# Loading five of 128 row tiles in pieces of 8, 112 and 8 rows in a DMA-bound rotation kernel

## Chip, cores and metric

One core of one Trainium2 chip. The metric is the device time of the whole kernel in microseconds. Of each kernel we quote the median of its runs and their range.

## The reference

```python
x = np.random.randn(8192, 8192).astype(np.float32)   # seeded
def reference(x, k):          # k = 1
    return np.rot90(x, k)
```

A matrix of 268 MB is read and 268 MB are written, turned by a quarter. There is no arithmetic.

## The kernel before

The input is cut into macro tiles of 1024 rows by 4096 columns (the last one into two of 512 rows). A macro tile is eight row tiles of 128 rows, 16 KB of each row. SP issues a load per row tile (128 in all); DVE reverses the columns of each 128-wide block on the way into chunk buffers; PE transposes blocks into PSUM; ACT copies PSUM to an output tile and issues the store.

```python
a_pool = ctx.enter_context(tc.tile_pool(name="a_pool", bufs=2))
r_pool = ctx.enter_context(tc.tile_pool(name="r_pool", bufs=63))
o_pool = ctx.enter_context(tc.tile_pool(name="o_pool", bufs=3))
# [cut]
def load(r0, rt, c0):
    nonlocal loads
    chunks = {}
    for t in range(rt):
        # [cut: a = a tile of 128 x 4096 from a_pool or, at the start, o_pool]
        loads += 1
        nc.sync.dma_start(
            out=a[:], in_=x[r0 + t * P : r0 + (t + 1) * P, c0 : c0 + W]
        )
        for j in range(W // CH):                 # CH = 512: 8 chunks
            ar = r_pool.tile([P, CH // P, P], dt, tag="ar")
            nc.vector.tensor_copy(out=ar[:], in_=...)   # columns reversed
            chunks[t, j] = ar
        yield chunks
```

There are 63 chunk buffers where a macro tile has 64 chunks, so the loads of the next macro tile follow closely on PE's transposes of this one.

## Time and profile before

| | before |
|---|---|
| time, median of 3 (range) | 1267.88 us (1267.56 to 1267.9) |
| span of the profiled run | 1265.8 us |
| bytes in and out | 268.44 + 268.44 MB |
| loads / stores | 128 / 129 |

The prediction below shows the lines of the page that carry the argument: the DMA row is full and the queues' shares add up to all 16 DMA engines. From the page, what the DMA engines moved in 40 equal slices of 31.6 us, and the two main groups of DMA issues with their KB and median us from issue to landing:

```profile
GB/s 398 426 429 429 428 429 429 428 431 427 429 429 429 428 430 429 429 428 429 429 429 428 429 421 430 427 430 429 423 429 428 418 429 428 428 429 425 428 422 334
...
out_dram<-ot ACTq DMA_DIRECT2D x127, 2048.0 KB, 25.6
a<-in_x_dram SPq DMA_DIRECT2D x128, 2048.0 KB, 16.7
```

428 to 430 GB/s is what this mix of loads and stores reaches when nothing is in its way. The table of stretches where the 25th tile will be loaded (the columns: stretch, its length, busy us and count of PE, PE weight loads, DVE, ACT and POOL, granted clock, DMA share, GB/s):

```profile
188.00:192.00 4.00, 0.00 (x0) 0.00 (x0) 0.00 (x0) 0.00 (x0) 0.00 (x0) 0.52 1.02 434
192.00:196.00 4.00, 1.12 (x4) 0.72 (x4) 1.87 (x6) 0.66 (x1) 0.00 (x0) 0.50 0.99 422
196.00:203.00 7.00, 5.74 (x32) 5.74 (x33) 0.91 (x3) 4.84 (x3) 0.00 (x0) 0.58 1.01 433
203.00:207.00 4.00, 3.78 (x34) 3.42 (x32) 2.78 (x8) 1.87 (x1) 0.00 (x0) 1.00 0.98 418
207.00:211.00 4.00, 1.69 (x16) 1.58 (x15) 0.00 (x0) 3.50 (x2) 0.00 (x0) 1.00 1.04 438
```

And the waits for PE (us in total, times, longest), with the stretch of 20 us where one of the macro tiles changes:

```profile
ACT ot L164 <- PE pt L143: 247.7, 43, 17.3
...
750.00:770.00 20.00, 12.63 (x90) 11.87 (x88) 5.55 (x16) 8.92 (x6) 0.00 (x0) 0.84 1.01 419
```

### The profile page before, as it was taken

To read this page: it belongs to the slowest core of one execution; us is meant where nothing else is said; L and a number is where in the kernel's file an instruction comes from. 1 tells how busy PE (TensorE), PEld (TensorE's weight loads), DVE (VectorE), ACT (ScalarE), POOL (GpSimd) and SP (SyncE) were. 2 spreads that over 40 slices of the span, in tenths; PEclk is the share of its full clock that TensorE was granted. 3 is DMA by queue.
4 is the path that set the end of the run, shared out by engine and by line. 5 is a ranking of instruction groups with operands and counts; after the bars stand their busy time and mean duration, and the time that the engine had idled before them with its cause. 6 is when DMAs were issued, how large, how long until landed. Compare 5 with 4: busy or idle time off the path is not lost.

```text
span 1265.8 us, 10385 instructions
## 1 busy us (share of the span) xinstructions
PE 685.3 (54%) x4096; PEld 639.3 (51%) x4096; DVE 355.3 (28%) x1024; ACT 467.8 (37%) x257; POOL 0.7 (0%) x6
## 2 busy tenths in 40 slices
PE   1555545555555554564555546566464655546573
PEld 1544444554445454554545545565454655545572
DVE  4423322232222322232222322233222332223210
ACT  0433334333343333433424334243442434324363
POOL 0000000000000000000000000000000000000000
PEclk9977877768777777777777776776767776767777
DMA  9999999999999999999999999999999999999998
GB/s 398 426 429 429 428 429 429 428 431 427 429 429 429 428 430 429 429 428 429 429 429 428 429 421 430 427 430 429 423 429 428 418 429 428 428 429 425 428 422 334
DMA packets 37057, 537.55 MB, mean 425 GB/s; under 512 B 4112, under 2 KB 4112, under 8 KB 4112
## 3 DMA queue, kind: packets, MB, share of 16 engines
q10 hardware_dynamic: 18576, 268.44, 50.0%
q1 hardware_dynamic: 18432, 268.44, 49.8%
q8 instruction: 32, 0.52, 0.2%
q14 instruction: 17, 0.14, 0.0%
HBM read 268.44 MB, written 268.44 MB: 424 GB/s over the span
## 4 chain that ended last, share of the span: by engine, by line
DMA 77%; ACT 8%; DVE 8%; PE 5%; issue 1%; ACTq 0%; DVEq 0%; SPq 0%
DMA a<-in_x_dram 48%; DMA out_dram<-ot 30%; ACT ot L164 8%; DVE ar L106 8%; PE pt L143 5%; ACTq L172 0%; DVEq L106 0%; ACTq L164 0%; SPq L101 0%
## 5 line engine op out<-in xcount | busy, mean ns | idle before, releaser
L143 PE MATMUL pt<-ident,ar 128*128 128x128 f32 x4096 | 685.3, 344 | 560.7 <-ACT ot L164 396.1
L143 PEld LDWEIGHTS pt<-ident,ar 128*128 128x128 f32 x4096 | 639.3, 183 | 606.5 <-ACT ot L164 433.2
L164 ACT COPY ot<-pt 128x2048 f32<-128x2048 f32 x256 | 466.5, 1869 | 755.5 <-DMA out_dram<-ot 506.3
L106 DVE COPY ar<-a 128x512 f32<-128x512 f32 x1024 | 355.3, 422 | 865.4 <-DMA a<-in_x_dram 827.9
L164 ACT ACT_TABLE_LOAD x1 | 1.3, 1283 | 25.6 <-DVE ar L106 25.6
masks.py:199 POOL TENSOR_SCALAR_AFFINE_SELECT ident<-ident 128x128 f32<-128x128 f32 x1 | 0.3, 292 | 0.1
masks.py:197 POOL MEMSET ident<- 128x128 f32 x1 | 0.2, 204 | 0.3 <-POOLq L212 0.3
L212 POOL MEMSET const-bfloat16-1.0<- 128x1 bf16 x1 | 0.1, 102 | 0.0
L212 POOL MEMSET const-uint8-127<- 128x1 uint8 x1 | 0.1, 102 | 0.0
L212 POOL MEMSET const-float32-0.0<- 128x1 f32 x1 | 0.1, 99 | 0.2 <-issue 0.2
L212 POOL MEMSET const-float32-1.0<- 128x1 f32 x1 | 0.1, 99 | 0.0
## 6 DMA issues: line engine op xcount, KB each, us to landing
a<-in_x_dram SPq DMA_DIRECT2D x128, 2048.0 KB, 16.7
out_dram<-ot ACTq DMA_DIRECT2D x127, 2048.0 KB, 25.6
out_dram<-ot ACTq DMA_DIRECT2D x2, 1024.0 KB, 14.9
```

What stands on the lines that cost most here:

```text
L106: nc.vector.tensor_copy(out=ar[:], in_=a[:, j * CH : (j + 1) * CH].rearrange("r (b m) -> r b m", m=P)[:, :, ::-1],)
L143: nc.tensor.transpose(ps[w // PW][:, PW - 1 - w % PW, t * P : (t + 1) * P], chunks[t, g * P // CH][:, g % (CH // P), :], ident,)
L164: nc.scalar.copy(o[:, G - PW - h : G - h, :], ps[h // PW])
L212: nc = _bacc.Bacc("TRN2", target_bir_lowering=False, num_devices=1)
```

## The change

With 8 + 112 + 8 rows, DMA engines 0 to 7 get nine rows of the tile and 8 to 15 get seven, in place of eight each; the prediction shows why. The intent, as far as it can be read, is to even out the DMA engines, which do not end together.

```diff
+EVERY = 25
+UNEVEN = [(0, 8), (8, P - 8), (P - 8, P)]
@@ in load()
             loads += 1
-            nc.sync.dma_start(
-                out=a[:], in_=x[r0 + t * P : r0 + (t + 1) * P, c0 : c0 + W]
-            )
+            for p0, p1 in UNEVEN if loads % EVERY == 0 else [(0, P)]:
+                r = r0 + t * P
+                nc.sync.dma_start(
+                    out=a[p0:p1, :], in_=x[r + p0 : r + p1, c0 : c0 + W]
+                )
```

## The prediction

> **What bounds the kernel now.** I read the page first: engine shares, slices, queues, chain.
>
> ```profile
> PE 685.3 (54%) x4096; PEld 639.3 (51%) x4096; DVE 355.3 (28%) x1024; ACT 467.8 (37%) x257; POOL 0.7 (0%) x6
> DMA  9999999999999999999999999999999999999998
> q10 hardware_dynamic: 18576, 268.44, 50.0%
> q1 hardware_dynamic: 18432, 268.44, 49.8%
> q8 instruction: 32, 0.52, 0.2%
> q14 instruction: 17, 0.14, 0.0%
> DMA 77%; ACT 8%; DVE 8%; PE 5%; issue 1%; ACTq 0%; DVEq 0%; SPq 0%
> ```
>
> No compute engine is over 54% busy. The DMA row is at 9 in 39 slices of 40, and the shares of the four queues add up to 100% of 16 engines' span: loads (q1) 49.8, stores (q10) 50.0, instruction fetches (q8, q14) 0.2. The chain of waits is 77% DMA. So the time is set by the 16 DMA engines, and work elsewhere is free as long as it feeds them.
>
> Next the table of stretches, to see where DMA is not full (columns: stretch, length, busy time and count of five engines, clock, DMA share, GB/s).
>
> ```profile
> 8.00:40.00 32.00, 7.77 (x28) 5.00 (x28) 18.45 (x54) 1.28 (x1) 0.00 (x0) 1.00 1.01 432
> 200.00:240.00 40.00, 22.54 (x158) 21.32 (x157) 11.10 (x32) 17.86 (x10) 0.00 (x0) 0.84 1.01 428
> 1180.00:1220.00 40.00, 23.64 (x130) 22.73 (x131) 11.75 (x36) 16.41 (x9) 0.00 (x0) 0.70 1.01 429
> 1220.00:1257.00 37.00, 22.37 (x192) 20.51 (x190) 0.72 (x3) 23.69 (x13) 0.00 (x0) 0.90 1.00 415
> 1257.00:1266.00 9.00, 0.00 (x0) 0.00 (x0) 0.00 (x0) 0.00 (x0) 0.00 (x0) 0.50 0.29 121
> ```
>
> Full from 8 to 1257 us, then 0.29 in the last 9: some engines are done while others work. That ragged end is all that balancing can win. I took it from the trace's own records. Each DMA posts 16 landings, one per engine. For the last store these come, after the first of them, at 0.0 (four), 0.1, 0.2, 1.0, 1.0, 1.7, 1.9, 1.9, 2.0, 2.1, 3.4, 5.6 and 6.5 us. The mean is 1.7 us, so perfect balance would save 6.5 - 1.7 = 4.8 us, 0.4%. No outcome near 2% faster is possible.
>
> Who is late? Packet records name no engine, but an engine's next packet starts 3 or 4 ns before its last ends, and each gets eight data packets and one semaphore write per DMA, so the records can be followed as 16 streams. My reconstruction gives: eight streams with the q8 fetches (32 of 16 KB, four each; this group ends with 0.2 to 3.4 us of lag); three of the other eight with all q14 fetches (7, 6 and 4 of 8 KB); five with none. The two that end last (6.5 and 5.6 us) are those with 7 and 6 q14 fetches. A q14 fetch takes 0.31 us and the packet after it about 1.2 instead of 0.61: 0.9 us. A q8 fetch takes 1.0 and the next packet 1.0: 1.4 us. The leaders sometimes run dry (near 675, 750, 907 and 986 us, about 0.1 us each time), because loads are released by the slowest engine's landing; the two laggards never wait. They are the bound.
>
> **What the Trainium skill says.** "DMA: Bandwidth & Descriptors", section "Why a DMA increments its semaphore by 16 and not by 1": the engine count is the largest number up to 16 that divides the slowest dimension, and on the hardware queues the lowest-numbered engines are taken. So 8 rows go to engines 0 to 7, one row each, and 112 rows to all 16, seven each. The trace of before agrees for 128 (16 landings per DMA, eight 16 KB packets each); 8 and 112 are not shown yet.
> "Runtime: NRT & Kernel Launch", section "Instruction fetch mechanics": instructions arrive in 16 KiB blocks by DMA queues of their own. The trace agrees: q8's 32 packets of 16 KB. It does not say which engines carry them.
> "SBUF — State Buffer", section "Door 1: The DMA port swizzle": partitions 0 to 3 share one port, 4 to 7 another, 120 to 123 and 124 to 127 two more, and four partitions alone got 27.6 GB/s. Before has no such case: each engine writes its own eight partitions of a 128-row tile (same DMA page, section "The descriptor swizzle"), and load packets show no slowing (0.611 us at the median and at the 90th percentile).
>
> **The change part by part.** Removed: five loads of 128 rows (the 25th, 50th, 75th, 100th and 125th; before, issued at 187, 433, 679, 925 and 1172 us). Added: 15 loads in their place. No PE, DVE or ACT instruction changes; the comparison of the two instruction orders shows only SP with more rows, 140 for 130. Costs:
> - Bytes. Engines 0 to 7 get 1 + 7 + 1 = 9 rows of such a tile, 8 to 15 get 7, instead of 8 each. One row is one packet of 0.611 us. Five tiles: +3.06 us on each of 0 to 7, -3.06 us on each of 8 to 15. Semaphore writes are 9 ns: ten more on 0 to 7, under 0.1 us.
> - Issue.
>
> ```profile
> L101 SPq DMA_DIRECT2D a<-in_x_dram x128: 327/328/534, 0.7 to 1201.1; - x128
> DMA to landing us min/median/max: 7.4/16.7/25.0
> ```
>
> Two more issues of 0.33 us put the last piece 0.66 us later. A load takes 16.7 us from issue to landing at a pace of one per 9.8 us, so its predecessor is still 6.9 us from landing at that moment. Hidden: 0.
> - Semaphores. The pieces use more of the eight DMA semaphores, so pieces two and three wait for earlier stores: for the first split tile those which before landed at 168.4 and 178.1 us, against an issue at 187.2. Checked for all DMAs of the program in the same way, no added wait ends after the old issue time. 0.
> - Writing 8 rows. Eight engines write to two ports. If the four on a port came together, 4 x 0.61 = 2.4 us would pass instead of 0.61, 1.8 us lost on each. But engines 0 to 7 are spread over a packet or more and alternate between loads and stores, so I estimate 0 to 1 us. The two laggards come 5 us after the others and can meet only each other: 0 to 0.6 us per piece, ten pieces, 0 to 6 us.
> - The 112 rows no longer lie engine by engine on its own port; a few packets may collide. Estimate 0 to 2 us over all five.
>
> So everything hangs on which half the two laggards are in. The change seems meant to relieve 8 to 15 of q8's fetches, which is the group of eight, 1.4 x 4 = 5.6 us against a relative shift of 2 x 3.06 = 6.1. In the very first load, the only moment when all engines start idle, the streams without q8 start early: places 1, 3, 4, 5, 7, 8, 9 and 11 of 16; the two laggards are third and fourth. If the order of start follows the engine number roughly, q8 is on 8 to 15 and the laggards, with their q14 fetches, are in 0 to 7. Then the change evens out the two halves on average and lengthens the two engines that end last: 1267.9 + 3.1 + (0 to 6) = 1271 to 1277.
>
> **The rivals.**
> (a) Laggards in 0 to 7, as just told. For: the order of first packets, and the author's choice of half. Against: that order is noisy (two q8 streams start second and sixth). +3.1 us without port contention, about +7 with it. I give it 0.6, half of that with contention.
> (b) q8 on 0 to 7, laggards in 8 to 15. The worst q8 engine has 3.4 + 3.06 = 6.5 us of lag, the laggards 6.5 - 3.06 = 3.4: the end stays at 6.5. 1268. Chance 0.15.
> (c) The halves are mixed, the laggards in 8 to 15 with the worst q8 engines. Best case: eight light engines in the lower half have at most 1.0 + 3.06 = 4.1 us, so the gain is 2.4; less when one with 2.1 us is among them (1.3). 1265.5 to 1266.6. For it: a kernel this tuned is seldom changed for nothing. Chance 0.25.
> (d) Full port contention on every piece, 1.8 us ten times: 1268 + 18 + 3 - 6 (the lead of the non-critical engines) = 1283. Against: the spread of the streams. It is the tail of (a).
>
> **Range and chances.** 0.3 x 1271 + 0.3 x 1275 + 0.15 x 1268 + 0.25 x 1266 = 1270.5. The low end, 1265.0, is just under the best of (c); the high end, 1278, takes in (a) with most of the contention. The repeats of before lie within 0.4 us, so noise adds nothing. Two per cent is 25 us: faster by that exceeds the 4.8 us there are; slower needs more than (d) in full. 0.01, 0.96, 0.03.
>
> **What would show it right or wrong.** The load queue should have 18432 packets plus the added semaphore writes; 268.44 MB as before; the first piece should post 8 landings, the second 16. If (a): the last store's landings keep two late streams, now some 9 us after the first unless leaders wait, and the DMA share of the last 9 us stays low. If (c): the spread of the last store shrinks to about 4 us. Contention: load packets of over 0.7 us in the five places, 8-row pieces slower than one packet time. If lanes matter after all: a DMA wait of SP over 12 us (the longest is 11.5 now), or DMA slices under 9 at 187 us and so on. I would be wrong altogether if the time fell below 1263, since that is more than the ragged end has to give, or rose past 1283.

## The result and the profile after

| | before | after |
|---|---|---|
| time, median of 6 (range) | 1267.82 us (1267.12 to 1267.9) | 1282.1 us (1279.8 to 1283.59) |
| ratio, 95% interval | 1 | 1.0111 (1.0098 to 1.0124) |
| span of the profiled run | 1265.8 us | 1280.1 us |

A ratio here and below is formed from the runs of the same rounds, so it is not quite the ratio of the medians quoted. The change costs 14.3 us, 1.1%. That is within 2%, but outside the predicted range of 1265 to 1278. The runs also scatter over 3.8 us, where those of before scatter over 0.8. All outputs are right.

The same lines of the page, after:

```profile
PE 688.8 (54%) x4096; PEld 640.3 (50%) x4096; DVE 355.2 (28%) x1024; ACT 468.1 (37%) x257; POOL 0.7 (0%) x6
GB/s 401 426 429 429 429 428 398 429 430 428 429 428 429 405 420 429 413 430 428 428 428 399 428 373 428 429 429 428 430 414 429 412 431 427 427 428 418 409 424 341
...
q1 hardware_dynamic: 18512, 268.44, 50.0%
q10 hardware_dynamic: 18576, 268.44, 49.7%
...
DMA 81%; DVE 12%; ACT 3%; PE 2%; issue 1%; ACTq 0%; DVEq 0%; SPq 0%
...
a<-in_x_dram SPq DMA_DIRECT2D x123, 2048.0 KB, 16.6
a<-in_x_dram SPq DMA_DIRECT2D x5, 1792.0 KB, 18.7
```

The kernel is still bound by DMA: the queues' shares still add up to 100%, and the chain is 81% DMA for 77%. The work is as the prediction said: the same bytes, and 18512 packets for 18432, which is the 10 x 8 added semaphore writes. But there are now dips in the GB/s row, and they can be turned into time. A slice is 32 us. The seventh covers 192 to 224 us, just where the 25th tile is loaded: 398 for 429 is (429 - 398) / 429 x 32 = 2.3 us lost. The 14th and 15th (the 50th tile) lose 1.8 + 0.7, the 22nd (the 75th tile) 2.2, the 30th (the 100th) 1.1, the 37th and 38th (the 125th) 2.3. The deepest dip, 373 in the 24th, is at no split tile; a macro tile changes there.

The table of stretches at the first split tile:

```profile
188.00:192.00 4.00, 0.00 (x0) 0.00 (x0) 0.00 (x0) 0.00 (x0) 0.00 (x0) 0.72 1.00 426
192.00:196.00 4.00, 1.11 (x4) 0.71 (x4) 2.05 (x7) 0.85 (x1) 0.00 (x0) 0.50 1.02 365
196.00:203.00 7.00, 5.72 (x37) 5.48 (x38) 0.72 (x3) 5.30 (x4) 0.00 (x0) 0.71 1.00 417
203.00:207.00 4.00, 3.15 (x29) 2.88 (x27) 0.00 (x0) 1.13 (x1) 0.00 (x0) 1.00 0.99 266
207.00:211.00 4.00, 0.00 (x0) 0.00 (x0) 2.77 (x8) 1.47 (x1) 0.00 (x0) 0.91 1.03 434
```

The DMA share stays at 0.99 to 1.03 in every row while the GB/s fall to 365 and then 266: the engines are not idle, their packets take longer. By the packet records the first piece of 8 rows passes at 192 to 196 us, the 112 rows up to 203 and the last 8 rows from 203 to 206.6. In the last stretch load packets take up to 1.57 us and store packets up to 1.26, where before each took 0.61 to 0.65.

Which engines? The split itself answers what the prediction could not know. The packet records name no engine, so this is a reconstruction, as in the prediction. Followed as 16 streams through the first split tile, a stream must carry one, seven and one row, or seven alone, so its half is given away. All streams with q8's fetches are in 8 to 15; all with q14's fetches, the two laggards among them, are in 0 to 7. That is the prediction's case (a). And the extra packet time from 203.2 to 206.6 us was 1.39 us on each engine of 0 to 7 and 1.48 us on each of 8 to 15, on the mean. Engines 8 to 15 have not a single row of that piece. They are held back as well, and their stores too. This does not hang on the reconstruction: all 16 load and store packets that began between 204.2 and 205.7 us took 1.11 us or more.

The waits for PE and a change of macro tile (the source lines have moved down by seven):

```profile
ACT ot L171 <- PE pt L150: 293.5, 50, 21.7
...
750.00:770.00 20.00, 9.49 (x56) 8.86 (x57) 5.90 (x18) 7.38 (x4) 0.00 (x0) 0.58 0.88 338
```

Here the DMA share itself drops, to 0.88: ACT waits longer for transposes (21.7 us for 17.3 at the longest), PE's clock is lower, and DMA runs dry for a while.

**An account of the 14 us.** Let the packets of a DMA engine take T us in all, on the mean of the 16. The end of the last packet is T plus what I call raggedness: the time in which engines have no packet, at the end, where they do not end together, and in dry spells before it. T can grow only by longer packets, since the packets' bytes are the same. I took the time of each load and store packet above its usual 0.613 us (in proportion for smaller ones), divided by 16, and split it into five windows of 40 us from the issue of each split tile (185, 430, 675, 920 and 1165 us) and the rest. From before to after the last packet ends 14.2 us later: T grows by 12.4, which is 9.7 in the five windows and 2.6 elsewhere (rounded), and raggedness by 1.7.

Two things have to be known of these parts. First, raggedness did not grow at the end. For the last store the latest landing lies 4.1 us after the mean of the 16, and before it was 4.8. What grew is idle time in the middle of the run: 2.8 us on the mean of the engines, for 0.3 before, and 2.5 of it lies between 740 and 780 us, where a macro tile changes. (Records overlap a little and the start shifts, so these do not add up to 1.7 exactly.) Second, packets are slow in two settings. Of the 9.7 us in the windows, 7.8 fall where loads and stores are both under way; 1.9, at the second and third split tile, fall where loads have few stores beside them (under a quarter of the bytes that start within 1 us). Outside of the windows nearly all of the growth is of this second kind. Loads alone are not slow as such: from 8 to 24 us, before any store, each packet takes 0.611 us. Why they are slow at a change of macro tile was not tested.

So the bulk is slowed packets at the five split tiles, about 2 us each on the mean (1.2 to 2.5). The experiments are about what slows them.

### The profile page after: what moved, and what is told of

Same layout as the page of the kernel before. It is cut to its first block, busy times and chain, and to the rows that moved or that the text cites. A ratio compares the mean times of both kernels' runs of the same rounds, so it can differ in the third digit from the quotient of the medians.

```text
span 1280.1 us, 10428 instructions
## 1 busy us (share of the span) xinstructions
PE 688.8 (54%) x4096; PEld 640.3 (50%) x4096; DVE 355.2 (28%) x1024; ACT 468.1 (37%) x257; POOL 0.7 (0%) x6
## 3 DMA queue, kind: packets, MB, share of 16 engines
q1 hardware_dynamic: 18512, 268.44, 50.0%
## 4 chain that ended last, share of the span: by engine, by line
DMA 81%; DVE 12%; ACT 3%; PE 2%; issue 1%; ACTq 0%; DVEq 0%; SPq 0%
DMA a<-in_x_dram 76%; DVE ar L113 12%; DMA out_dram<-ot 4%; ACT ot L171 3%; PE pt L150 2%; ACTq L179 0%; DVEq L113 0%; SPq L108 0%; ACTq L171 0%
## 5 line engine op out<-in xcount | busy, mean ns | idle before, releaser
L171 ACT ACT_TABLE_LOAD x1 | 1.3, 1283 | 25.6 <-DVE ar L113 25.6
## 6 DMA issues: line engine op xcount, KB each, us to landing
a<-in_x_dram SPq DMA_DIRECT2D x123, 2048.0 KB, 16.6
```

Source lines behind the costliest of these rows:

```text
L171: nc.scalar.copy(o[:, G - PW - h : G - h, :], ps[h // PW])
```

## The experiments

**Theories.** *Ports*: a whole tile loads fast because each engine writes to a port of SBUF of its own (the skill's map, as the prediction cites it); rows that arrive elsewhere crowd ports and hold back every engine. *Rivals*: the count of loads with their issue and semaphores; the rows read from memory; the place of the five tiles in the program; the shift of bytes to the laggards; dry spells set off by late loads.

### Extra 8-row loads into a spare tile: room, near, spread, near_far

These add ten loads of 8 rows to the kernel before, whose own loads stay whole. The spare tile needs room, so the number of chunk buffers had to go down to 55; `room` is the control with that alone.

```diff
-    r_pool = ctx.enter_context(tc.tile_pool(name="r_pool", bufs=63))
+    r_pool = ctx.enter_context(tc.tile_pool(name="r_pool", bufs=55))
+    scr = consts.tile([P, W], dt)                     # not in room
@@ near: ahead of and behind every 25th load
+    nc.sync.dma_start(out=scr[0:8, :],     in_=x[r : r + 8, c0 : c0 + W])
+    nc.sync.dma_start(out=scr[P - 8 : P, :], in_=x[r + P - 8 : r + P, c0 : c0 + W])
@@ spread: the same rows of x, each to a port of its own
+    out=scr[0:32:4, :]      out=scr[96:P:4, :]
@@ near_far: as near, but rows of x far from each other
+    in_=x[r : r + P : 16, ...]   in_=x[r + 8 : r + P : 16, ...]
```

> Control, no part of the change in it: the kernel before with 55 instead of 63 buffers for reversed chunks, to free 16 KB per partition for the next three runs. All theories: within 4 us of before (1267.8), since DMA stays full; its difference from before is to be subtracted from nothing but is the base of the next three.

> The control plus ten extra loads of 8 rows into a spare tile (five to partitions 0 to 7, five to 120 to 127, adjacent source rows), nothing taken from engines 8 to 15. Each gives engines 0 to 7 one more packet: 10 x 0.61 = 6.1 us on the engines that end last, if those are in 0 to 7. Theory P (eight engines writing into two SBUF ports hold up the whole DMA system, the 2.3 us per split tile seen in the trace): control + 6 + about 11 = +17 us. Theory S (the source rows, adjacent rows of x, collide in the memory): also +17. Theory M (it is the 112-row middle piece, or the issue, semaphores and small size of the pieces): +6.

> As near, but the 8 rows go to every fourth partition (0, 4, ... 28 and 96, 100, ... 124), so that eight engines write eight ports; same source rows, same number of DMAs. Theory P: control + 6 us, no slow packets. Theory S: as near, +17. Theory M: as near, +6.

> As near (partitions 0 to 7 and 120 to 127), but the source rows are 16 apart. Theory P: as near, control + 17. Theory S: less than near, about +6. Theory M: +6.

| | median (range) us | ratio to before |
|---|---|---|
| room | 1289.51 (1289.0 to 1289.85) | 1.017 |
| near | 1304.47 (1303.94 to 1306.05) | 1.0287 |
| spread | 1298.53 (1298.15 to 1299.79) | 1.0243 |
| near_far | 1304.13 (1302.94 to 1304.89) | 1.0285 |

The control alone lost 21.8 us, where at most 4 was expected: with eight buffers fewer, DMA slows down at every change of macro tile, some 80 us apart. By the account above, 19.3 us of it are longer packets and only 2.9 idle time. The longer packets lie mostly where loads have few stores beside them: from 292 to 296 us 78 load packets and no store packet began, and they took 0.88 us on the mean. Two stretches of room with a DMA share of 0.97 (before has 419 GB/s at shares of 1.01 and 1.00 there):

```profile
750.00:770.00 20.00, 7.26 (x34) 6.47 (x35) 5.22 (x15) 4.96 (x3) 0.00 (x0) 0.51 0.97 411
990.00:1010.00 20.00, 5.57 (x24) 4.78 (x25) 5.21 (x15) 3.63 (x2) 0.00 (x0) 0.50 0.97 411
```

So DMA is not at its full rate in the base of this set, and the scheduler moved the extra loads forward, to 40 to 198 us, in all three alike. Only differences within the set can be used. near less spread is 5.9 us: same loads, rows, bytes and engines, and only the destination's partitions differ. That speaks for ports, 0.6 us a piece, about half of what the port theory had said (near 17 us above the control and spread 6; they are 15.0 and 9.0 above). near_far less near is -0.3 us: for these 8-row loads, which rows of memory are read does not matter. The packets bear both out. From 40 to 200 us, where the extra loads lie, packets took longer than usual by 7.8 us (mean of 16 engines) in near and 7.6 in near_far, but 2.9 in spread and 2.2 in room.

### Small extra loads: tiny

Ten extra loads of 8 rows and only 512 bytes a row, into a small spare tile, to price the loads and semaphores without bytes.

```diff
+    scr = consts.tile([P, P], dt)
+    nc.sync.dma_start(out=scr[0:8, :], in_=x[r : r + 8, c0 : c0 + P])   # ahead, every 25th
+    nc.sync.dma_start(out=scr[P - 8 : P, :], in_=x[r + P - 8 : r + P, c0 : c0 + P])
```

> The kernel before plus ten loads of 8 rows by 512 bytes into a spare tile: the issues, semaphores and half-used engine sets of the pieces, without their bytes or their port time. Port and byte theories: within 1 us of before. If the mere presence of the extra DMAs on the queue (issue, semaphore turn, start-up of a piece) costs: +3 us or more.

1275.62 us (1274.38 to 1277.77), ratio 1.006. This control failed. The scheduler moved all ten loads into the first 100 us, and with one spare tile each waited for others, as the waits of SP's queue show:

```profile
SPq L105 <- DMA scr<-in_x_dram: 31.0, 4, 11.1
SPq L113 <- DMA scr<-in_x_dram: 5.1, 3, 3.9
```

The loads behind them came late, and between 60 and 100 us DMA ran dry (a share of 0.90, 361 GB/s). In the five windows there was nothing (-0.1 us against before). It prices its own waits, not those of the change, whose SP queue waits at most 11.5 us, as before.

### Cut by columns: cols

Three loads for each of the five tiles, but all 128 rows in each, so that every engine keeps its own eight partitions.

```diff
-UNEVEN = [(0, 8), (8, P - 8), (P - 8, P)]
+CUTS = [(0, 1024), (1024, 3072), (3072, W)]
-            for p0, p1 in UNEVEN if loads % EVERY == 0 else [(0, P)]:
+            for q0, q1 in CUTS if loads % EVERY == 0 else [(0, W)]:
-                    out=a[p0:p1, :], in_=x[r + p0 : r + p1, c0 : c0 + W]
+                    out=a[:, q0:q1], in_=x[r : r + P, c0 + q0 : c0 + q1]
```

> The five tiles in three pieces by columns (1024, 2048, 1024 wide, all 128 rows each): as many DMAs, issues and semaphores as the change, no shift of bytes, each engine on its own port. If issue, semaphores or the mere number of pieces cost anything: up to +11 us on before. Port theory and byte theory: within 1 us of before, 1267 to 1269.

1274.13 us (1273.45 to 1274.79), ratio 1.0049: 6.3 us more than before, so the expectation of next to nothing missed. But the loss is elsewhere. At the split there is none, and at changes of macro tile there is:

```profile
192.00:199.00 7.00, 2.54 (x11) 2.14 (x12) 2.78 (x8) 3.34 (x2) 0.00 (x0) 0.50 1.01 427
199.00:207.00 8.00, 7.57 (x59) 7.06 (x57) 2.20 (x6) 5.49 (x4) 0.00 (x0) 0.89 1.00 421
...
270.00:290.00 20.00, 10.31 (x60) 9.22 (x61) 8.33 (x24) 7.38 (x4) 0.00 (x0) 0.60 0.96 375
```

Slowed packets in the five windows: +0.1 us. Its packets of 4 and 8 KB take turns with store packets of 16 KB, so the load gets less than half of the DMA time; the tile landed at 211.4 us instead of 203.8, and dry spells came after (ACT's longest wait for transposes 28.4 us). So three loads instead of one do not slow packets. And a load that is late for any reason costs some us later.

### Four row cuts with less crowding or no shift: pieces16, low16, two_ports, even32

```diff
# pieces16: 16 + 96 + 16 rows, all engines in each piece
+UNEVEN = [(0, 16), (16, P - 16), (P - 16, P)]
# the others have pieces (first, end, step) and slices p0:p1:by
# low16: 8 + 8 + 112 rows
+UNEVEN = [(0, 8, 1), (8, 16, 1), (16, P, 1)]
# two_ports: even rows, odd rows of the first 16, then 112
+UNEVEN = [(0, 16, 2), (1, 16, 2), (16, P, 1)]
# even32: even rows, odd rows of the first 32 (16 engines each), then 96; no shift of bytes
+UNEVEN = [(0, 32, 2), (1, 32, 2), (32, P, 1)]
```

> The five tiles in pieces of 16, 96 and 16 rows: all 16 engines get 1 + 6 + 1 rows, so no shift of bytes between the halves; but each 16-row piece is written by 16 engines into four ports. Port theory: no byte term, contention as in the change or more: +8 to +15 us, with slow packets on all engines. If only the uneven share (and not the contention) cost: 0.

> The change with its two 8-row pieces side by side (rows 0 to 7, 8 to 15, then 16 to 127): same number of DMAs and same bytes per engine; each 8-row piece still has four engines on each of two ports. Port theory: as the change, +13 to +16 us on before. If the place of the pieces (before and after the middle) matters more than the ports: clearly different from +14.

> As low16, but the first piece takes the even rows of 0 to 15 and the second the odd ones: only the order of rows within the first 16 differs, the bytes, counts and engines are the same, and each piece has two engines on each of four ports instead of four on two. Port theory: the hot port takes 1.2 instead of 2.4 us, so the excess over one packet time (0.6 instead of 1.8 us) falls to a third: +14 becomes +6 to +9. If ports do not matter: as low16.

> Even rows of 0 to 31, odd rows of 0 to 31, then 32 to 127: 16, 16 and 96 rows, so all engines share alike, with two engines per port as in two_ports. If my byte term is right (engines 0 to 7 hold the two that end last, one row more per tile costs 0.61 us): two_ports minus 3 us. If bytes do not matter: as two_ports.

Results are in the table at the end of this section: 9.9, 11.8, 10.4 and 7.3 us more than before. pieces16 has no shift of bytes and still loses most of what the change loses, so the shift is not the bulk. two_ports against low16, with the four partitions of a port shared by two engines instead of four, lost 2.2 us less in the windows but only 1.4 less in time, and the ranges of their times overlap. two_ports and even32 crowd their small pieces alike, two engines to a port, and differ in the shift: 1278.43 - 1275.28 = 3.15 us, where the prediction's byte term is 3.06; their ranges just touch (1277.4 and 1278.43). The agreement does not isolate the shift: in the profiled runs the two end 5.0 us apart, and that difference lies in longer packets elsewhere (2.6 us) and in a dry spell of two_ports between 740 and 760 us (2.2 us), while in the windows two_ports has 1.0 less.

### More of it, and fewer fetches: ten, fewfetch

```diff
# ten: the changed kernel with ten split tiles
-EVERY = 25
+EVERY = 12
# fewfetch: the kernel before with half as many DVE copies and buffers of twice the size
-CH = 512
+CH = 1024
-    r_pool = ... bufs=63
+    r_pool = ... bufs=31
```

> The change on ten tiles (every 12th) instead of five. Byte shift plus contention are both per tile: 10 x (0.61 + 2.3) = +29 us on before, 1296 to 1298, twice the change's +14.3. If some of the +14.3 is paid once or is a state of the pipeline (bunching of loads and stores): clearly less than twice.

> Not a part of the change: the kernel before with reversal copies of 1024 columns instead of 512 (512 instead of 1024 VectorE instructions, 31 buffers of twice the size). If the two engines that end last are late by instruction fetches of 8 KB (7 and 6 of 0.9 us each), some of which are VectorE's, it drops 3 to 5 of those and the end comes 2 to 4 us sooner: 1264 to 1266. If the lag has another cause, or the coarser buffers stall the loads: 1268 or more.

ten: 1293.15 us (1292.08 to 1296.94), +25.3 us, 1.77 times the change's 14.3 and some 4 us short of the 29 expected. The cost goes up with the number of split tiles, if not quite in proportion. fewfetch: 1291.65 us (1289.92 to 1295.8), ratio 1.0192. It was to test whether instruction fetches make the laggards, and it failed: 31 large buffers slow DMA down as room's 55 small ones do (19.0 us of longer packets, 4.7 of idle time). Whether fetches alone make the laggards was not tested.

### The same tiles at another place: phase

```diff
-            for p0, p1 in UNEVEN if loads % EVERY == 0 else [(0, P)]:
+            for p0, p1 in UNEVEN if loads % EVERY == 12 else [(0, P)]:
```

> The changed kernel with the same three pieces for the 12th, 37th, 62nd, 87th and 112th tile in place of the 25th and so on. Port theory: ten crowded pieces again, 10.7 + 3.1 us, and a few us of dry spells that depend on the place: before + 12 to 17, 1280 to 1285 us. Rival (most of the 14.3 us is an accident of where the splits fall against the stages of the program): outside of that, under + 10 or over + 19.

1281.57 us (1281.23 to 1281.66), ratio 1.0107: +13.5 us for +14.3. The cost is no accident of which tiles are split.

### The split tile in five loads, crowded or not: five_near, five_own

The cleanest pair: the first 32 rows in four loads of 8, then 96. Number, bytes, engines, buffers and issue are the same; only the order of 32 partitions among four loads differs, and with it the rows of x that are read together, which made no difference to near_far.

```diff
# five_near
+UNEVEN = [(8 * i, 8 * i + 8, 1) for i in range(4)] + [(32, P, 1)]
# five_own: every fourth row, so each engine of a piece has a port alone
+UNEVEN = [(i, 32, 4) for i in range(4)] + [(32, P, 1)]
```

> The five tiles in five loads: rows 0 to 7, 8 to 15, 16 to 23, 24 to 31, then 32 to 127. Engines 0 to 7 get 4 + 6 = 10 rows, 8 to 15 get 6, so the bytes cost five times 2 x 0.61 = 6.1 us. Port theory (two crowded ports slow all engines, about 1.1 us for each 8-row piece as in the changed kernel): 20 pieces, 22 us, and 1 to 4 us of semaphore waits and dry spells: before + 28 to 33, 1296 to 1301 us. Rival (the number of pieces, waits and dry spells cost, not the ports): the same as five_own within 3 us.

> As five_near, but the four pieces take every fourth row of the first 32, so that each of the eight engines of a piece writes a port alone. Same loads, bytes, engines and semaphores. Port theory: 6.1 us for bytes, 0 to 4 for waits and dry spells, no crowding: before + 6 to 10, 1274 to 1278 us, that is 18 to 26 us under five_near. Rival: the same as five_near within 3 us, whatever both are.

five_near 1283.74 us (1281.42 to 1284.3), ratio 1.0118; five_own 1280.34 us (1280.21 to 1281.33), ratio 1.0099. The difference has the sign of the port theory, and the ranges do not overlap, but it is 3.4 us and not 18 to 26; the rival had said within 3. Their absolute cost holds more than the pieces: in both, loads waited for earlier stores (22.5 us in all in five_near and 20.1 in five_own, 9.1 at the longest), which the change's did not. Before has 426 GB/s in both stretches of this table; five_near, then five_own:

```profile
192.00:199.00 7.00, 2.34 (x10) 1.95 (x11) 2.77 (x8) 3.15 (x2) 0.00 (x0) 0.50 1.03 391
199.00:207.00 8.00, 7.79 (x50) 7.55 (x49) 0.00 (x0) 4.22 (x3) 0.00 (x0) 0.70 1.01 297
```

```profile
192.00:199.00 7.00, 3.03 (x13) 2.63 (x14) 2.78 (x8) 3.63 (x2) 0.00 (x0) 0.50 0.99 419
199.00:207.00 8.00, 7.60 (x57) 6.91 (x55) 0.00 (x0) 3.73 (x2) 0.00 (x0) 0.87 1.02 326
```

In the first stretch the small pieces are under way. With a port each, the longest load packet took 0.618 us and the longest store packet 0.631: nothing at all is slowed. Crowded, load packets took up to 1.37 us and store packets up to 1.14. In the second stretch the 96 rows pass, and now both kernels are slow, 326 and 297 GB/s. So the theory as I had it, with the 8-row pieces as the culprits, was too narrow: a large piece does it too. That led to the last three.

### Large pieces only, and another order: two96, halves, ends_first

```diff
# two96: six, then two rows to each of 16 engines
+UNEVEN = [(0, 96), (96, P)]
# halves: four rows to each of 16 engines, twice
+UNEVEN = [(0, 64), (64, P)]
# ends_first: the pieces of the change, small ones first
+UNEVEN = [(0, 8), (P - 8, P), (8, P - 8)]
```

> The five tiles in two pieces of 96 and 32 rows, six and two rows to each of 16 engines: no 8-row piece, no shift of bytes, one more load per tile. If the 8-row pieces carry the cost: before + 0 to 3. If rows off their own port do, whatever the size of the piece: before + 5 to 9, as even32, whose last piece is this one's first.

> The five tiles in two pieces of 64 rows, four to each of 16 engines; each half of the tile lies on 8 ports, two engines to a port throughout. If only 8-row pieces on two ports are dear: before + 0 to 3. If rows off their own port are: before + 6 to 12, more than two96, since every row is crowded by two and the ports of one half hold back all loads when loads run alone.

> The changed kernel's three pieces in another order: rows 0 to 7, 120 to 127, then 8 to 119. Rows, bytes, engines and ports as in the changed kernel. If the small pieces carry the cost wherever they stand: before + 12 to 16, as the changed kernel. If the last piece was dear because it is last (the engines without a row of it are already in the next tile, two of them on the same two ports): before + 8 to 11. If the 112 rows carry it: before + 12 to 16 too, with the slow packets after the two small pieces.

two96: 1278.18 us (1273.43 to 1278.64), ratio 1.0076. halves: 1280.31 us (1276.5 to 1283.84), ratio 1.0097. ends_first: 1279.66 us (1279.12 to 1280.95), ratio 1.0098. Neither of the first two has an 8-row piece or gives one engine more bytes than another, and each has just one load more per tile. two96, then halves, at the first split tile:

```profile
192.00:199.00 7.00, 3.09 (x13) 2.69 (x14) 2.78 (x8) 3.64 (x2) 0.00 (x0) 0.50 0.99 379
199.00:207.00 8.00, 7.18 (x56) 6.66 (x55) 1.57 (x5) 3.64 (x2) 0.00 (x0) 0.90 1.01 418
```

```profile
192.00:199.00 7.00, 3.29 (x14) 2.89 (x15) 2.78 (x8) 3.64 (x2) 0.00 (x0) 0.50 0.99 351
199.00:207.00 8.00, 6.72 (x56) 6.20 (x54) 1.25 (x4) 3.64 (x2) 0.00 (x0) 0.95 1.01 418
```

379 and 351 GB/s at a DMA share of 0.99. In halves, the more crowded of the two, there is more of it: 10.2 us in the five windows, as much as in the changed kernel. The order of the pieces matters little: ends_first is 2.4 us below the changed kernel's median, from separate rounds.

### All row cuts in one account

Change against before in us: of the median; of the end of the last packet in the profiled run; and the three parts of that end.

| kernel | pieces of the five tiles (rows) | median | end | slow packets, five windows | longer packets elsewhere | raggedness (idle time) |
|---|---|---|---|---|---|---|
| cols | 128, 128, 128 (by columns) | 6.3 | 6.8 | 0.1 | 4.1 | 1.8 |
| even32 | 16, 16, 96 | 7.3 | 6.2 | 5.6 | 1.6 | -1.2 |
| two96 | 96, 32 | 10.5 | 11.0 | 5.7 | 4.0 | 1.2 |
| halves | 64, 64 | 12.7 | 8.8 | 10.2 | 0.6 | -2.1 |
| pieces16 | 16, 96, 16 | 9.9 | 12.7 | 11.6 | 1.2 | -0.3 |
| two_ports | 8, 8, 112 | 10.4 | 11.2 | 4.6 | 4.2 | 2.4 |
| low16 | 8, 8, 112 | 11.8 | 12.6 | 6.8 | 4.7 | 1.1 |
| ends_first | 8, 8, 112 | 12.0 | 11.5 | 7.6 | 3.3 | 0.5 |
| the change | 8, 112, 8 | 14.3 | 14.2 | 9.7 | 2.6 | 1.7 |
| five_own | 8, 8, 8, 8, 96 | 12.3 | 13.6 | 6.9 | 3.6 | 3.1 |
| five_near | 8, 8, 8, 8, 96 | 15.7 | 16.6 | 8.5 | 4.0 | 3.9 |

A profiled run can lie some us from its kernel's median (halves most), so single us in this table mean nothing. Three things stand out. Every cut by rows loses 4.6 to 11.6 us to slow packets at the split tiles, and the cut by columns nothing to speak of (0.1, counted against the usual time of its 4 and 8 KB packets). Longer packets elsewhere, mostly where macro tiles change, add 0.6 to 4.7. Raggedness is -0.1 on the mean of the five kernels without a shift of bytes, 1.4 with the change's shift (four kernels) and 3.5 with twice that (two). This goes with the shift, but it holds dry spells, and cols has 1.8 without any shift, so it does not show that the shift is the cause.

The expectations hit the times of pieces16, phase and, just, ends_first, and the difference of even32. The port theory had low16 (13 to 16 us), ten (29) and five_near (28 to 33) too dear, and two_ports (6 to 9), two96 (5 to 9), halves (6 to 12) and five_own (6 to 10) too cheap. It has the right sign in both pairs that were made for it, near with spread and five_near with five_own; sizes it does not give.

## Why the prediction was wrong, and where right

**Bound, size of the gain, right.** The kernel stayed bound by DMA, and nothing was gained at the ragged end that shows in the time: the last store's landings still lie 5.7 us apart (6.5 before).

**Bytes and semaphore writes: the count right, the price open.** 8 rows take 8 engines and 112 take 16, as the 18512 packets show, and by the reconstruction the laggards are in 0 to 7, case (a). That the shift costs 3.1 us is not shown. two_ports less even32 gives 3.15 us, but in dry spells and longer packets as much as anything. And the sign that the prediction named for (a), two late streams "now some 9 us after the first unless leaders wait", did not come: it is 5.7 us. Whether leaders waited instead was not measured.

**Issue and lanes, right.** In the changed kernel the three issues of the first split tile come at 186.86, 187.25 and 187.62 us, 0.76 us for the two that were added (0.66 predicted), and the longest DMA wait of SP's queue is still 11.5 us.

**Wrong: the size of port contention.** Two terms of the sum failed. One is "Writing 8 rows": "The two laggards come 5 us after the others and can meet only each other: 0 to 0.6 us per piece, ten pieces, 0 to 6 us." The other is "The 112 rows no longer lie engine by engine on its own port; a few packets may collide. Estimate 0 to 2 us over all five." Both took a collision to be a matter between the engines that collide, so that the laggards, late and alone, would escape. The runs show in its place that all engines lose: 1.39 and 1.48 us in the two halves at the last piece of the first split, loads and stores alike, 9.7 us on the mean of 16 engines over the five windows, 7.8 of it with loads and stores both under way. Laggards are not spared when everyone is slowed. And two96 (5.7 us) and halves (10.2) show that large pieces off the usual mapping are dear too, three and five times what the second term allowed. Half of the weight of case (a) went to no contention at all; no row cut that was run was without it.

Case (d) gave 1283 and was put down as the tail. Its number came close, but by luck, for its mechanism was not what happened either: it took the small pieces alone as slow, at 1.8 us each, and subtracted a lead of the other engines, which they do not have if they are slowed too.

**Missing: what late loads set off.** Another 2.6 us, by the account, are longer packets outside of the windows, mostly at changes of macro tile, and dry spells there are the idle time that grew. The prediction had no term for either. cols shows that they need no contention: 4.1 us of longer packets there, and dry spells, with no slow packet at the split. With 63 chunk buffers for 64 chunks there is little slack: room lost 21.8 us with eight fewer.

**What stays open.** How the 9.7 us divide between the 8-row pieces and the 112 rows: at the first split tile they lie at the small pieces (0.7 us at the first, 1.45 at the last, 0.2 between), at five_own's they lie at the large one. The cost of a crowded piece is no constant: 0.6 us each in near, but only 0.17 each in five_near (3.4 us for twenty). For pieces of 64 and 96 rows the memory side is a rival that no run excludes: which rows of x the engines read at the same time changes together with the partitions, and near_far tested 8-row loads alone. What path the engines share was not observed; that ports are what crowds is inferred from which destinations are slow (five_own against five_near, spread against near, cols against all row cuts) together with the skill's map. No version was found that beats the kernel before. The chips of separate rounds were not compared beyond their runs of before, which agree within 0.4 us.

## What to carry to other kernels

Where loads and stores fill the DMA engines, leave a load in the shape in which each engine writes its own partitions: moving 3 us of bytes from one half of the engines to the other cost 14 us, mostly because loads off that mapping slowed the loads and stores of all engines. A DMA share of 1.0 does not show this; read it with the GB/s of the same stretch, and sum packet times. Before one evens out engines, find out which of them are late: here the half that was given more held the two that ended last.

## What the Trainium skill lacked or had wrong

- "SBUF — State Buffer", section "Door 1: The DMA port swizzle": it states that 64 partitions reach only 8 ports and no more bandwidth than 32. The runs agree in kind (halves: 351 GB/s in all where before has 426). It lacks that the loss is not confined to the crowded load: at the change's last 8-row piece, engines with no row of it lost 1.48 us against 1.39 on its own, and store packets rose from 0.61 to as much as 1.26 us.
- "DMA: Bandwidth & Descriptors", section "Back-pressure in remote DMA": it tells of a clogged port that holds back other engines and other queues of the same engine, for transfers between cores. The runs show the same outward effect in plain loads from memory on one core, with the numbers of the point above; that a clogged port is behind it was not seen.
- "DMA: Bandwidth & Descriptors", section "The descriptor swizzle": it gives the partitions of each engine for 128 rows, and sends the reader elsewhere for other shapes, where only the number of engines and which they are is told, not their partitions. What such a shape costs beside full streams of other loads and stores is on no page: 1 to 2 us of longer packets per tile of 2 MB here, for pieces of 96 + 32 or 64 + 64 rows.
- "DMA: Bandwidth & Descriptors", section "Why a DMA increments its semaphore by 16 and not by 1": right; 10 x 8 and 20 x 8 writes were added for 8-row loads, and 16 for each large one (18512 packets in the change and in two96, 18592 in five_own).
- "Runtime: NRT & Kernel Launch", section "Instruction fetch mechanics": it gives fetches as 16 KiB blocks and calls the cost of crossing one "mostly hidden", which is said of the engine that runs the instructions. Here one queue's fetches are of 8 KB, and it lacks what a fetch costs the DMA engine that carries it: 1.4 us (16 KB) or 0.9 us (8 KB) in this kernel full of DMA. No page says which engines carry them: by the reconstruction, the 16 KB fetches were all on 8 to 15, the 8 KB ones on three of 0 to 7.
